# A projection stage whose written order is kept on VectorE alone, the other engines left to the list scheduler

## The chip, the core and the metric

The kernel runs on one core of a Trainium2 chip. Its time is the device time of one execution in microseconds (us). The engines are PE (TensorE: matmuls and transposes), DVE (VectorE), ACT (ScalarE), POOL (GpSimd) and SP (SyncE, which issues every DMA here). Each engine runs its own instructions in the order in which they stand in its program, and semaphores make one engine wait for another. So the time depends on two things that the arithmetic does not fix: the order on each engine, and what each instruction has to wait for.

## What is computed

One layer of a hybrid decoder trunk, for 2048 tokens of 1024 channels, in float32:

```python
mod = silu(c) @ W_ada + b_ada          # shift, scale, gate; for the mixer and for the MLP
h = rms_norm(x) * (1 + scale1) + shift1
p = h @ W_in                           # q_a k_a v_a | q_m k_m v_m o_m | u_s v_s | f_a i_m f_m
y = concat(forgetting_attention(q_a, k_a, v_a, f_a),       # 8 heads of 64
           sigmoid(o_m) * rms_norm(mlstm(q_m, k_m, v_m, i_m, f_m)),   # 4 heads of 64
           spatial_gating(gelu(u_s), gelu(v_s)))           # 4 groups of 64
x = x + gate1 * (y @ W_out)
x = x + gate2 * conv_ffn(rms_norm(x) * (1 + scale2) + shift2)
```

The change touches the product `h @ W_in` and the work that is done beside it.

## The kernel before

The program has four stages, one after another: the **projection** (`h @ W_in`, from the start to about 775 us), attention, the product with `W_out`, and the convolutional MLP.

**Precision.** A float32 operand is split into a rounded high part and a low rest (`hh` and `hl` of h, `wh` and `wl` of a weight), and `mm3` (lines 53 to 56) makes three matmuls of each product. The high part of a weight is a cast on ACT (line 652), the low part a subtraction on DVE (line 653).

**The projection's loop.** The list `steps` has 14 entries: seven blocks of columns of `W_in` for the first 1024 tokens, and the same seven for the other 1024. In the order of the first half they are `km` (keys of the mLSTM and all gates, 272 columns), `qo`, `vm`, `us`, `K`, `Q` and `V`. A block makes eight accumulators `acc` of 24 matmuls each, 112 in the whole stage; here they are counted from 0. They lie in three PSUM buffers, in the last step in two. While a block runs, the weights of the next are loaded (`wr`, three buffers, line 640 for the DMA) and split into `wh` and `wl` (eleven buffers each).

**The first block** (`first_block`, n = 0) is written apart, because h does not exist yet. x is loaded in tiles `xt` of 128 tokens; `norm_sums` squares each tile on ACT (line 558, two halves), sums on DVE (559, 561), takes a power on POOL (128), and line 571 scales the tile on DVE. `first_mod` sums the modulation on DVE (`modacc`, 442 and 444) and POOL (`modown`, 438 to 440) and transposes the sums on PE (447), and lines 453 to 455 give shift and scale for four of the eight channel tiles. `make_h` then goes over the eight channel tiles k: four transposes on PE (605), `h` on ACT (609), `hh` and `hl` on DVE (610, 611). Behind this block `mlstm_setup` (890 to 908) makes small constants: `sel`, `maskb`, `maskT`, `rmask`. `maskb` and `maskT` come from two POOL tiles (895 to 900).

**Side work.** From n = 1 on, generators ("lanes") hand out small pieces of other work between the products: the rest of the modulation (`rest_of_mod`, 500 and 502, with `columns_or_row`, 517 and 527), the recurrent mLSTM (`mlstm`, `mlstm_end`), the spatial gating (`level`, `spatial`), the transposes of normalised keys and queries (`turn`, 841 to 855: a sum, a power on POOL, `qn`, a transpose `trp`, then `qhi` and `qlo`), and for the second half a `refill` of the x tiles. In the last step (block `V`) the first eight attention scores run as a lane: `sp` on PE (206, 210), `L` with its minimum on DVE (212), an exponential on ACT (223). Block `V` itself evicts each accumulator in two halves, a cast on ACT (829) and a subtraction on DVE (830) into `vhl`, and stores them (831) from three buffers `q2k`.

**What sets the order.** Two mechanisms. A list scheduler places the instructions of an engine by its own estimate of when their inputs are ready; outside a `manual_schedule` it does so for all five. Inside `manual_schedule` (entered at n = 1 and left behind the loop) the engines named, that is PE, DVE, ACT and POOL, keep exactly the order in which the program is written, that is the order in which the lanes hand out their pieces. SP is not named, so DMAs are placed by the scheduler throughout. The first block lies outside and is placed by the scheduler on all engines.

Of the kernel before, what the change touches and what calls it, by code (L numbers as in the profile page):

```python
# [33 lines left out]
def trunk(  # L34
# [18 lines left out]
    def mm3(ps, lh, ll, rh, rl, start, stop, resume=False):  # L53
        T.matmul(ps, lh, rh, start=start, stop=False, skip_group_check=resume)  # L54
        T.matmul(ps, lh, rl, start=False, stop=False, skip_group_check=resume)  # L55
        T.matmul(ps, ll, rh, start=False, stop=stop, skip_group_check=resume)  # L56

# [417 lines left out]
    def rest_of_mod():  # L475
# [15 lines left out]
        for col in cols:  # L491
            acc = pool.tile([P, 512], F32, name="modacc", tag="t2k")
            for k in range(KT):
# [5 lines left out]
                if k == 0:  # L499
                    V.tensor_scalar(acc, st, cs[:, 0:1], None, op0=ALU.mult)  # L500
                else:
                    V.scalar_tensor_tensor(acc, st, cs[:, k : k + 1], acc, op0=ALU.mult, op1=ALU.add)
# [9 lines left out]
    def columns_or_row(acc, col):  # L512
# [4 lines left out]
        V.tensor_tensor(acc[0:1, :], acc[0:1, :], brow, op=ALU.add)  # L517
# [7 lines left out]
        else:  # L525
# [3 lines left out]
            if kind == 3:  # L529
                V.tensor_copy(sh2[:, sl], ps[:, 0:4])  # L530
            else:
                V.scalar_tensor_tensor(
                    a2[:, sl], ps[:, 0:4], 1.0, gf[:, half * 4 : half * 4 + 4], op0=ALU.add, op1=ALU.mult
                )
# [80 lines left out]
    class Weights:  # L615
# [28 lines left out]
        def cast(self):  # L644
# [8 lines left out]
            self.eng.tensor_tensor(lo, self.raw[k], hi.bitcast(F32), op=ALU.subtract)  # L653
# [74 lines left out]
    def use_km(tt, ps):  # L728
# [3 lines left out]
        V.tensor_tensor(gates[:, tt % 8, 64:72], ps[:, 256:264], gbias[:, 0:8], op=ALU.add)  # L732
        V.tensor_tensor(
# [3 lines left out]
        )  # L737
# [24 lines left out]
    def use_vm(tt, ps):  # L762
        t = pool.tile([P, 256], F32, name="ev", tag="ev")
        V.tensor_copy(t, ps[:, 0:256])
# [15 lines left out]
    def level(tt, i, t, u, vn):  # L780
        mu = pool.tile([P, 4], F32, name="mu", tag="mu")
        V.tensor_reduce(mu, t, axis=AX.X, op=ALU.add)
        V.tensor_scalar(mu, mu, 1.0 / 64, None, op0=ALU.mult)
        V.tensor_tensor(t, t, bc(mu, 2, 64), op=ALU.subtract)
# [12 lines left out]
    def spatial(tt, u, vn):  # L797
        y = pool.tile([P, 4, 256], F32, name="sy", tag="t4k")
        mixed = []
        for g in range(4):  # L800
# [6 lines left out]
            if g % 2:  # L807
                for g_ in (g - 1, g):
                    sl = slice(g_ * 64, g_ * 64 + 64)
                    V.tensor_tensor(y[:, :, sl], mixed[g_], bc(gsgu[:, sl], 1, 4), op=ALU.mult)  # L810
                    V.scalar_tensor_tensor(
                        y[:, :, sl], y[:, :, sl], bs_col[:, g_ : g_ + 1], u[:, :, sl], op0=ALU.add, op1=ALU.mult
                    )
# [11 lines left out]
    def use_v(tt, ps):  # L825
        for h0 in (0, 4):
# [3 lines left out]
            V.tensor_tensor(t[:, :, 1, :], p3, t[:, :, 0, :].bitcast(F32), op=ALU.subtract)  # L830
            dma(v_d[tt * P : (tt + 1) * P, h0 : h0 + 4], t.bitcast(F32).rearrange("p h e d -> p h (e d)"))

    def use_qk(which):
# [5 lines left out]
        def turn(tt, ps, sq):  # L839
            ss = pool.tile([P, 8], F32, name="ss", tag="ss")  # L840
            V.tensor_reduce(ss, sq.rearrange("p (h d) -> p h d", h=8), axis=AX.X, op=ALU.add)
            V.tensor_scalar(ss, ss, 1.0 / 64, EPS, op0=ALU.mult, op1=ALU.add)
# [1012 lines left out]
```

## Time and profile before

| What | Number |
|---|---|
| Median of 3 runs | 2672.68 us (2670.3 to 2673.54) |
| Profiled execution, its own time | 2675.71 us |
| Its span, from first to last instruction | 2674.0 us |
| Mean granted TensorE clock | 0.988 |

The rows of the profile are shown with the prediction, where they are used. Times in them are microseconds from the start of the span. A row of the timeline has the start, the duration, the engine, the line of the kernel, the operation, output and inputs by their names in the program, and in brackets the idle time of the engine ahead of it with the instruction that ended that idle time. A row of the windows has, for a stretch of time, the busy time of PE, its weight loads (PEld), DVE, ACT and POOL, each with its count of instructions, then the granted TensorE clock (1.00 is full), the share of time that the DMA engines were busy, and GB/s. A row of the waits says which engine waited at which line for which engine's result, for how long in all, how often, and at most.

### The profile page before, as it was taken

How to read it: one execution, taken by the hardware profiler on the slowest of the kernel's cores; microseconds unless marked ns; L12 is line 12 of the kernel's file. 1: busy time of each engine (PE TensorE's matmuls, PEld its weight loads, DVE VectorE, ACT ScalarE, POOL GpSimd, SP SyncE). 2: the span in 40 equal slices, each digit the busy share in tenths (PEclk: the TensorE clock that was granted, in tenths of full speed). 3: DMA queues.
4: the chain of work that ended last, by engine and by line, in shares of the span. 5: the costliest groups of instructions: out<-in, count | busy, mean ns of one | idle time of the engine just before them, and what ended most of it. 6: DMA issues, size and time to landing. Idle time of an engine off the chain costs nothing.

```text
span 2674.0 us, 36818 instructions
## 1 busy us (share of the span) xinstructions
PE 2580.6 (97%) x12761; PEld 2128.9 (80%) x12761; DVE 1992.1 (75%) x3432; ACT 1285.4 (48%) x2442; POOL 415.6 (16%) x550
## 2 busy tenths in 40 slices
PE   5899999999899999999999999999999999999999
PEld 5788787888777877777877888888888888888787
DVE  5555656455448888876749888887988887898797
ACT  3333334333248788874436544444444444444443
POOL 4012210022236566640000000000000000000000
PEclk9899999999999999999999999999999999999999
DMA  7533556424554444536742222228222225748533
GB/s 257 154 117 91 150 152 184 132 70 123 138 171 123 115 133 125 136 98 229 276 142 72 90 84 84 82 84 294 89 85 82 84 79 206 267 148 308 177 101 116
DMA packets 297683, 377.52 MB, mean 141 GB/s; under 512 B 31118, under 2 KB 189676, under 8 KB 295448
## 3 DMA queue, kind: packets, MB, share of 16 engines
q1 hardware_dynamic: 297496, 375.16, 44.4%
q8 instruction: 101, 1.65, 0.3%
q14 instruction: 86, 0.70, 0.1%
HBM read 274.34 MB, written 100.74 MB: 140 GB/s over the span
## 4 chain that ended last, share of the span: by engine, by line
PE 74%; DVE 11%; DMA 5%; ACT 4%; issue 4%; POOL 1%; SPq 0%; DVEq 0%; ACTq 0%; POOLq 0%
PE ub L54 10%; PE ub L56 10%; PE ub L55 10%; PE acc L54 5%; PE acc L56 5%; PE acc L55 5%; PE db L55 4%; PE db L56 4%; PE db L54 4%; PE tp L259 3%; PE sp L206 3%; PE op L245 2%; PE op L246 2%; DVE wspl L1599 2%; DMA x_d<-x 1%
## 5 line engine op out<-in xcount | busy, mean ns | idle before, releaser
L54 PE MATMUL acc<-wh,hh 128*128 128x512 f32 (+2 forms) x768 | 290.8, 379 | 10.9 <-DVE vhl L830 5.3
L55 PE MATMUL acc<-wl,hh 128*128 128x512 f32 (+2 forms) x768 | 277.5, 361 | 4.5 <-POOL wl L677 3.4
L54 PE MATMUL ub<-T,wsph 128*128 128x512 f32 x704 | 274.3, 390 | 5.8 <-ACT wsph L1467 5.8
L56 PE MATMUL acc<-wh,hl 128*128 128x512 f32 (+2 forms) x768 | 278.1, 362 | 0.4 <-DVE hl L611 0.4
L56 PE MATMUL ub<-T,wspl 128*128 128x512 f32 x704 | 273.8, 389 | 0.4 <-DVE wspl L1468 0.4
L55 PE MATMUL ub<-T,wsph 128*128 128x512 f32 x704 | 273.9, 389 | 0.0
L55 PE MATMUL db<-wspl,wsph 128*128 128x512 f32 x616 | 240.4, 390 | 2.2 <-DVE wspl L1599 2.2
L56 PE MATMUL db<-wsph,wspl 128*128 128x512 f32 x616 | 239.6, 389 | 0.0
L54 PE MATMUL db<-wsph 128*128 128x512 f32 x616 | 238.3, 389 | 0.3 <-ACT wsph L1598 0.3
L1467 ACT CAST wsph<-S 128x512 fp32r<-128x512 f32 x176 | 109.7, 623 | 228.6 <-PE ub L55 162.5
L263 DVE TENSOR_TENSOR plo<-tp,phi 128x512 fp32r<-128x512 f32 (+1 forms) x320 | 186.8, 607 | 35.9 <-ACT phi L262 34.0
L54 PE MATMUL ub<-B,wsph 128*128 128x512 f32 x528 | 207.3, 393 | 2.6 <-ACT wsph L1467 2.6
L56 PE MATMUL ub<-B,wspl 128*128 128x512 f32 x528 | 207.0, 392 | 0.8 <-DVE wspl L1468 0.8
L55 PE MATMUL ub<-B,wsph 128*128 128x512 f32 x528 | 207.1, 392 | 0.0
L223 ACT ACTIVATE L<-L,nm 128x1024 f32<-128x1024 f32 (+2 forms) x192 | 172.5, 902 | 32.1 <-DVE nm L212 30.8
L259 PE MATMUL tp<-ident,L 128*128 128x128 f32 x1088 | 178.6, 276 | 5.2 <-DVE vhl L830 1.9
L262 ACT CAST phi<-tp 128x512 fp32r<-128x512 f32 (+1 forms) x320 | 160.1, 521 | 46.0 <-PE tp L259 44.7
L54 PEld LDWEIGHTS acc<-wh,hh 128*128 128x128 f32 x768 | 148.3, 193 | 32.3 <-issue 6.6
L206 PE MATMUL sp<-kk,q 128*128 128x512 f32 (+3 forms) x640 | 168.4, 374 | 2.3 <-DVE nm L212 1.2
L228 POOL TENSOR_SCALAR L<-L,rs 128x1024 f32<-128x1024 f32 (+2 forms) x192 | 167.2, 881 | 11.2
L1598 ACT CAST wsph<-act 128x512 fp32r<-128x512 f32 x132 | 82.2, 623 | 179.0 <-PE db L55 162.6
L55 PEld LDWEIGHTS acc<-wl,hh 128*128 128x128 f32 x768 | 148.2, 193 | 25.1 <-POOL wl L677 3.7
(344 smaller groups left out, 6025.8 us busy)
## 6 DMA issues: line engine op xcount, KB each, us to landing
w<-in_w_up_dram SPq DMA_DIRECT2D x88, 512.0 KB
wd<-in_w_down_dram SPq DMA_DIRECT2D x176, 256.0 KB
wa<-in_w_ada_dram SPq DMA_DIRECT2D x96, 256.0 KB
act_d<-yc SPq DMA_DIRECT2D x44, 512.0 KB
act<-act_d SPq DMA_DIRECT2D x44, 512.0 KB
wr<-in_w_in_dram SPq DMA_DIRECT2D x76, 256.0 KB
q<-q_d SPq DMA_DIRECT2D x128, 128.0 KB
hc_d<-hl SPq DMA_DIRECT2D x28, 512.0 KB
```

The costliest lines, as they stand in the source:

```text
L54: T.matmul(ps, lh, rh, start=start, stop=False, skip_group_check=resume)
L55: T.matmul(ps, lh, rl, start=False, stop=False, skip_group_check=resume)
L56: T.matmul(ps, ll, rh, start=False, stop=stop, skip_group_check=resume)
L206: T.matmul(sp[:, b : b + bw], q2[n][:, qs], kk[:, s0 + b : s0 + b + bw], start=n == 0, stop=n == 1 and not last)
L223: A.activation(L[c], L[c], AF.Exp, bias=nm[:, n - 1 : n], scale=-1.0, accum_out=rs[:, c : c + 1])
L228: G.tensor_scalar(t, t, rs[:, 0:1], 1.0, op0=ALU.mult, op1=ALU.mult)
L245: T.matmul(op[:, c0:], vv[:, j, :], hi[:, c0:], start=(j == 0), stop=False)
L259: T.transpose(tp[:, i * P : (i + 1) * P], rows[i][j // 8][:, (j % 8) * P : (j % 8 + 1) * P], ident)
L262: A.copy(hi[:, c0:], tp[:, c0:])
L263: V.tensor_tensor(lo[:, c0:], tp[:, c0:], hi[:, c0:].bitcast(F32), op=ALU.subtract)
L1467: A.copy(hi, src)
L1598: A.copy(hi, v)
```

## The change

The `manual_schedule` goes. In its place most VectorE instructions of the projection are wrapped in `O(...)`, which ties an instruction behind the one that was written just before it on the same engine, whether that is wrapped or not. The scheduler then places PE, ACT and POOL freely through the whole projection, and DVE in written order as far as it is wrapped. Not wrapped are `make_h` (610, 611), `norm_sums` (559, 561), the scaling in `norm_x` (571), `mlstm_setup`, the copy in `small_setup` and the scores (212): these may move ahead of what is written before them. Since the wrapping also holds for the first block, some of its DVE instructions are now tied too. The sets of instructions are the same in both programs; behind the projection the order is the same too.

```diff
+    O = tc.keep_in_program_order
...
-                    V.tensor_scalar(acc, st, cs[:, 0:1], None, op0=ALU.mult)
+                    O(V.tensor_scalar(acc, st, cs[:, 0:1], None, op0=ALU.mult))
...
-            self.eng.tensor_tensor(lo, self.raw[k], hi.bitcast(F32), op=ALU.subtract)
+            O(self.eng.tensor_tensor(lo, self.raw[k], hi.bitcast(F32), op=ALU.subtract))
...
-        V.tensor_tensor(gates[:, tt % 8, 64:72], ps[:, 256:264], gbias[:, 0:8], op=ALU.add)
+        O(V.tensor_tensor(gates[:, tt % 8, 64:72], ps[:, 256:264], gbias[:, 0:8], op=ALU.add))
...
-            V.tensor_tensor(t[:, :, 1, :], p3, t[:, :, 0, :].bitcast(F32), op=ALU.subtract)
+            O(V.tensor_tensor(t[:, :, 1, :], p3, t[:, :, 0, :].bitcast(F32), op=ALU.subtract))
...
-            V.tensor_tensor(n, ps.rearrange("p (h d) -> p h d", h=8), bc(ss, 2, 64), op=ALU.mult)
+            O(V.tensor_tensor(n, ps.rearrange("p (h d) -> p h d", h=8), bc(ss, 2, 64), op=ALU.mult))
...
-    in_order = tc.manual_schedule(
-        engines={mybir.EngineType.PE, mybir.EngineType.DVE, mybir.EngineType.Activation, mybir.EngineType.Pool}
-    )
     for n, (half, i) in enumerate(steps):
         if n == 1:
-            in_order.__enter__()
             lane(in_turn(log_gates(), iter((6,)), small_setup()), 2)
...
-    in_order.__exit__(None, None, None)
```

The same wrapping stands around the VectorE lines of `columns_or_row`, `use_vm`, `level`, `spatial`, `turn`, `log_gates`, `mlstm`, `mlstm_end` and the scaling in `normed`. Lines behind 57 are two higher in the changed kernel.

**First place: the norms and the constants around the first block.** ACT before, from the second half's `h` to the squares. Tile numbers are the program's own: `xt_564` to `xt_570` are the x tiles 4 to 7, `acc_440`, `453` and `466` are accumulators 0, 1 and 2.

```order
L730 COPY ev_584<-acc_440 128x256
L730 COPY ev_604<-acc_453 128x256
L596 COPY wT_289<-mp_628 128x512
L730 COPY ev_649<-acc_466 128x256
L558 ACTIVATE jk_655,st_654<-xt_564 128x512
L558 ACTIVATE jk_657,st_654<-xt_564 128x512
L558 ACTIVATE jk_664,st_663<-xt_566 128x512
L558 ACTIVATE jk_666,st_663<-xt_566 128x512
L558 ACTIVATE jk_673,st_672<-xt_568 128x512
L558 ACTIVATE jk_675,st_672<-xt_568 128x512
L558 ACTIVATE jk_682,st_681<-xt_570 128x512
L558 ACTIVATE jk_684,st_681<-xt_570 128x512
```

ACT in the changed kernel at the same place; the same x tiles are `xt_562` to `xt_568`, the accumulators `438`, `451`, `464`, and `wr_599`, `644`, `713` are the first three raw weights of the next block.

```order
L654 CAST wh_837<-wr_599 128x512
L560 ACTIVATE jk_653,st_652<-xt_562 128x512
L560 ACTIVATE jk_655,st_652<-xt_562 128x512
L654 CAST wh_874<-wr_644 128x512
L654 CAST wh_911<-wr_713 128x512
L611 ACTIVATE h32_523<-mp_518,sh1_90,a1_89 128x512
L611 ACTIVATE h32_534<-trp_529,sh1_90,a1_89 128x512
L611 ACTIVATE h32_545<-trp_540,sh1_90,a1_89 128x512
L611 ACTIVATE h32_556<-mp_551,sh1_90,a1_89 128x512
L560 ACTIVATE jk_662,st_661<-xt_564 128x512
L598 COPY wT_289<-mp_626 128x512
L732 COPY ev_582<-acc_438 128x256
```

Three weight casts and the squares of x tiles 4 and 5 moved ahead of the `h` and the evictions; in the changed program four squares are left behind the third eviction (`ev_647`), where there were eight.

DVE before, at the end of the first block, with the constants of `mlstm_setup` between two low parts of weights:

```order
L653 TENSOR_TENSOR wl<-wr,wh 128x512 x4
L732 TENSOR_TENSOR gates<-acc,gbias 128x8
L733 TENSOR_TENSOR gates<-acc,gbias 128x2x4
L893 COPY sel<-ident 4x128 x4
L897 CAST maskb<-m_978 128x128
L901 CAST maskT<-maskf 128x512
L902 MEMSET rmask 4x512
L903 MEMSET rmask 4x4
L907 COPY sel<-ident 4x64 x4
L653 TENSOR_TENSOR wl<-wr,wh 128x512
```

DVE in the changed kernel, some fifty rows earlier: the last sums of the modulation (L444 and L446), and the masks between them.

```order
L444 TENSOR_SCALAR modacc<-wa,cs 128x512
L446 SCALAR_TENSOR_TENSOR modacc<-wa,cs,modacc 128x512 x6
L561 TENSOR_TENSOR st<-st 128x1
L899 CAST maskb<-m_976 128x128
L446 SCALAR_TENSOR_TENSOR modacc<-wa,cs,modacc 128x512
L563 TENSOR_SCALAR st<-st 128x1
L903 CAST maskT<-maskf 128x512
L446 SCALAR_TENSOR_TENSOR modacc<-wa,cs,modacc 128x512
L573 TENSOR_SCALAR xt<-xt,st 128x1024
L455 TENSOR_TENSOR sh_90<-mps,colA 128x4
L456 TENSOR_TENSOR a_89<-mps,colA 128x4
L457 SCALAR_TENSOR_TENSOR a_89<-a_89,colA 128x4
```

`maskb` and `maskT` moved ahead of the last two sums and of the shift and scale that `h` waits for; `rmask` and `sel` moved to the program's first rows. The scaling of x tile 4 (L573) moved ahead of the shift and scale too.

**Second place: the products behind the second set of transposes.** PE before, where accumulator 4 (`acc_811`) follows the last transpose of x:

```order
L605 MATMUL trp_800<-ident_74,xt_568 128x128
L605 MATMUL trp_800<-ident_74,xt_570 128x128
L54 MATMUL acc_811<-wh_346,hh_729 128x272
L55 MATMUL acc_811<-wl_347,hh_729 128x272
L56 MATMUL acc_811<-wh_346,hl_730 128x272
L54 MATMUL acc_811<-wh_352,hh_740 128x272
L55 MATMUL acc_811<-wl_353,hh_740 128x272
L56 MATMUL acc_811<-wh_352,hl_741 128x272
L54 MATMUL acc_811<-wh_358,hh_751 128x272
```

PE in the changed kernel, where `acc_809` and `acc_846` are accumulators 4 and 5:

```order
L607 MATMUL trp_798<-ident_74,xt_562 128x128
L607 MATMUL trp_798<-ident_74,xt_564 128x128
L607 MATMUL trp_798<-ident_74,xt_566 128x128
L607 MATMUL trp_798<-ident_74,xt_568 128x128
L54 MATMUL acc_809<-wh_364,hh_760 128x272
L55 MATMUL acc_809<-wl_365,hh_760 128x272
L56 MATMUL acc_809<-wh_364,hl_761 128x272
L55 MATMUL acc_846<-wl_347,hh_727 128x272
L54 MATMUL acc_809<-wh_370,hh_771 128x272
L55 MATMUL acc_809<-wl_371,hh_771 128x272
L56 MATMUL acc_846<-wh_346,hl_728 128x272
L54 MATMUL acc_846<-wh_352,hh_738 128x272
```

The matmuls of accumulators 4 and 5 now stand mixed with each other and with the transposes, as each channel tile of h is made. Before, accumulator 5 begins behind the last matmul of 4.

**Third place: the end of the projection.** PE before: `acc_6976` is accumulator 107 (block `V`), `sp_6990` the first attention score.

```order
L56 MATMUL acc_6976<-wh_6717,hl_3695 128x512
L54 MATMUL acc_6976<-wh_6748,hh_3745 128x512
L55 MATMUL acc_6976<-wl_6749,hh_3745 128x512
L56 MATMUL acc_6976<-wh_6748,hl_3746 128x512
L206 MATMUL sp_6990<-kk_6829,q_6835 128x512
L206 MATMUL sp_6990<-kk_6829,q_6838 128x512
L206 MATMUL sp_6990<-kk_6829,q_6835 128x128
L206 MATMUL sp_6990<-kk_6829,q_6838 128x128
L210 LDWEIGHTS identb_95
L210 MATMUL sp_6990<-maskb_97,identb_95 128x128
L54 MATMUL acc_6976<-wh_6757,hh_3769 128x512
L55 MATMUL acc_6976<-wl_6758,hh_3769 128x512
```

PE in the changed kernel: `acc_6941` is accumulator 106, `sp_6988` and `sp_7021` are the first two scores.

```order
L56 MATMUL acc_6941<-wh_6781,hl_3817 128x512
L54 MATMUL acc_6941<-wh_6806,hh_3827 128x512
L55 MATMUL acc_6941<-wl_6807,hh_3827 128x512
L56 MATMUL acc_6941<-wh_6806,hl_3828 128x512
L208 MATMUL sp_6988<-kk_6827,q_6833 128x512
L208 MATMUL sp_7021<-kk_6827,q_6833 128x512
L208 MATMUL sp_6988<-kk_6827,q_6836 128x512
L208 MATMUL sp_6988<-kk_6827,q_6833 128x128
L208 MATMUL sp_6988<-kk_6827,q_6836 128x128
L212 LDWEIGHTS identb_95
L212 MATMUL sp_6988<-maskb_97,identb_95 128x128
L208 MATMUL sp_7021<-kk_6827,q_6836 128x512
```

All eight scores, 40 rows, now stand between accumulators 106 and 107; before, each stood inside one of the accumulators 107 to 111, behind half of its matmuls.

DVE before, at the same place (L830 is the low half of an eviction of block `V`, L212 a score with its minimum, in two rows):

```order
L855 SCALAR_TENSOR_TENSOR qlo<-trp,gq_94,qhi 128x512
L830 TENSOR_TENSOR vhl<-acc,vhl 128x4x64 x2
L212 ISA L,nm<-sp,nf 128x640
L212 ISA nm 128x1
L830 TENSOR_TENSOR vhl<-acc,vhl 128x4x64 x2
L212 ISA L,nm<-sp,nf 128x768
L212 ISA nm 128x1
L212 ISA L,nm<-sp,nf 128x896
L212 ISA nm 128x1
L830 TENSOR_TENSOR vhl<-acc,vhl 128x4x64 x2
L212 ISA L,nm<-sp,nf 128x1024
L212 ISA nm 128x1
```

DVE in the changed kernel (L832 and L214 now):

```order
L214 ISA L,nm<-sp,nf 128x1024
L214 ISA nm 128x1
L214 ISA L,nm<-sp,nf 128x128
L214 ISA nm 128x1
L214 ISA L,nm<-sp,nf 128x256
L214 ISA nm 128x1
L214 ISA L,nm<-sp,nf 128x384
L214 ISA nm 128x1
L832 TENSOR_TENSOR vhl<-acc,vhl 128x4x64
L857 SCALAR_TENSOR_TENSOR qlo<-trp,gq_94,qhi 128x512
L832 TENSOR_TENSOR vhl<-acc,vhl 128x4x64
L214 ISA L,nm<-sp,nf 128x512
```

Rows 3 to 8 here are the last of seven scores that stand ahead of the second eviction half of accumulator 105 (L832 in row 9), behind which accumulator 107 finds its buffer free; before, evictions and scores took turns.

More of the change, by code (lines that the diff above doesn't have):

```diff
@@ L499, in rest_of_mod @@
                 if k == 0:
-                    V.tensor_scalar(acc, st, cs[:, 0:1], None, op0=ALU.mult)
+                    O(V.tensor_scalar(acc, st, cs[:, 0:1], None, op0=ALU.mult))
                 else:
-                    V.scalar_tensor_tensor(acc, st, cs[:, k : k + 1], acc, op0=ALU.mult, op1=ALU.add)
+                    O(V.scalar_tensor_tensor(acc, st, cs[:, k : k + 1], acc, op0=ALU.mult, op1=ALU.add))
                 if k == KT - 1:
@@ L516, in columns_or_row @@
         yield 2
-        V.tensor_tensor(acc[0:1, :], acc[0:1, :], brow, op=ALU.add)
+        O(V.tensor_tensor(acc[0:1, :], acc[0:1, :], brow, op=ALU.add))
         yield 1
@@ L809, in spatial @@
                     sl = slice(g_ * 64, g_ * 64 + 64)
-                    V.tensor_tensor(y[:, :, sl], mixed[g_], bc(gsgu[:, sl], 1, 4), op=ALU.mult)
-                    V.scalar_tensor_tensor(
+                    O(V.tensor_tensor(y[:, :, sl], mixed[g_], bc(gsgu[:, sl], 1, 4), op=ALU.mult))
+                    O(V.scalar_tensor_tensor(
                         y[:, :, sl], y[:, :, sl], bs_col[:, g_ : g_ + 1], u[:, :, sl], op0=ALU.add, op1=ALU.mult
-                    )
+                    ))
                 yield 1
@@ L926, in mlstm @@
         yield 1
[L927 to L929 removed]
+        O(V.tensor_copy(mp_[:, 0:1], mcar))
+        O(V.tensor_tensor_scan(m, lf, psI, mcar, op0=ALU.add, op1=ALU.max))
+        O(V.tensor_tensor_scan(b, rmask, lf, 0.0, op0=ALU.mult, op1=ALU.add))
         yield 1
[L931 to L935 removed]
+        O(V.tensor_tensor(e, m, b, op=ALU.subtract))
+        O(V.tensor_copy(mp_[:, 1:5], r4(m)[:, :, P - 1]))
+        O(V.tensor_tensor(a, psI, b, op=ALU.subtract))
+        O(V.tensor_tensor(r4(R[0:4]), bc(mp_[:, 0:4], 2, P), r4(e), op=ALU.subtract))
+        O(V.tensor_copy(mcar, mp_[:, 4:5]))
         A.mul(ne, e, -1.0)
@@ L1099, in normed @@
         scale = lambda pair, sts: [
-            V.tensor_scalar(xt, xt, st, None, op0=ALU.mult) for xt, st in zip(pair, sts)
+            O(V.tensor_scalar(xt, xt, st, None, op0=ALU.mult)) for xt, st in zip(pair, sts)
         ]
```

90 lines of the change are left out of this document (41 added, 49 removed).

## The prediction, made before the changed kernel ran

> **What bounds the kernel now.** First the page's totals and its chain, then windows by stage, then who waits on PE.
>
> ```profile
> span 2674.0 us, 36818 instructions
> PE 2580.6 (97%) x12761; PEld 2128.9 (80%) x12761; DVE 1992.1 (75%) x3432; ACT 1285.4 (48%) x2442; POOL 415.6 (16%) x550
> PE 74%; DVE 11%; DMA 5%; ACT 4%; issue 4%; POOL 1%; SPq 0%; DVEq 0%; ACTq 0%; POOLq 0%
> ...
> 0.00:100.00 100.00, 65.51 (x352) 57.59 (x353) 59.16 (x134) 40.22 (x89) 34.63 (x50) 0.91 0.59 198
> 100.00:750.00 650.00, 626.70 (x3395) 524.49 (x3395) 354.62 (x797) 221.57 (x435) 110.25 (x92) 0.98 0.46 135
> 750.00:800.00 50.00, 46.90 (x234) 36.88 (x233) 25.12 (x57) 24.47 (x57) 19.85 (x32) 0.97 0.54 158
> 800.00:2674.00 1874.00, 1841.48 (x8784) 1509.91 (x8782) 1553.24 (x2447) 999.09 (x1864) 250.89 (x376) 1.00 0.43 140
> ```
>
> PE is busy for 97% of the span and makes 74% of the chain that ends last. The change leaves every matmul in place, so it can only win or lose time in which PE is idle or at a lower clock. The first row of the windows (0 to 100 us) has 34.5 us of idle PE, the second (100 to 750) 23.3 us, at clock 0.98. From 800 us on the order is unchanged and PE runs at 1.00. So the whole effect lies in the first 780 us. What PE waits for there (0 to 800 us, the waits that the moved rows touch):
>
> ```profile
> PE acc L54 <- DVE vhl L830: 5.3, 2, 3.5
> PE acc L54 <- DVE qn L846: 5.1, 1, 5.1
> PE mp L521 <- DVE modacc L517: 3.9, 2, 2.2
> PE trp L850 <- DVE qn L846: 3.2, 2, 2.3
> PE acc L56 <- DVE wl L653: 2.3, 1, 2.3
> PE mp L527 <- DVE colC L551: 1.4, 1, 1.4
> PE acc L55 <- DVE wl L653: 1.0, 1, 1.0
> PE acc L54 <- ACT wh L652: 0.8, 1, 0.8
> ```
>
> They are short and scattered, and each is a place where one engine's order made a result late. There is no single large stall to remove.
>
> **First block, the start of h.** Three timelines, POOL, DVE and PE, around 50 us:
>
> ```profile
> 45.83 3.10 POOL L589 TENSOR_SCALAR_AFFINE_SELECT wsn<-wsn 128x128 f32<-128x128 f32 x4
> 70.91 0.20 POOL L895 MEMSET m<- 128x128 f32 x1
> ...
> 72.12 0.29 POOL L900 TENSOR_SCALAR_AFFINE_SELECT maskf<-maskf 128x128 f32<-128x128 f32 x1
> 43.70 5.08 DVE L444 SCALAR_TENSOR_TENSOR modacc<-wa,cs,modacc 128x512 f32<-128x512 f32 x5
> 58.39 0.40 PE L56 MATMUL acc<-wh,hl 128*128 128x272 f32 x1 [0.21 <-DVE hl L611]
> ```
>
> Here the change loses. `maskT` now stands on DVE ahead of the last modulation sum and needs POOL's four mask instructions, which took 70.91 to 72.41 = 1.5 us and come behind `wsn`, done at 48.93. So `maskT` can start at 50.4. With itself (0.4, below) and one sum (5.08 / 5 = 1.0) the sums end at 51.8 instead of 48.78, 3.0 late. Twelve of the sixteen transposes that stood between the sums and h are now ahead of them, which gives back about 0.8. I take h 2.2 us late: the last `hl` of these four channel tiles, at 58.3 before, comes at 60.5.
>
> **First block, the norms of the next x tiles.** DVE's first norm sum, its last scaling and the last `hl`; ACT's squares as groups (63 to 69 us); PE's first matmul of the next block:
>
> ```profile
> 64.96 0.16 DVE L559 TENSOR_TENSOR st<-st 128x1 f32<-128x1 f32 x1 [0.99 <-ACT jk L558]
> ...
> 71.00 0.75 DVE L571 TENSOR_SCALAR xt<-xt,st 128x1024 f32<-128x1024 f32 x1 [0.66 <-POOL st L128]
> ...
> 81.04 0.69 DVE L611 TENSOR_TENSOR hl<-h,hh 128x512 fp32r<-128x512 f32 x1
> L558 ACT ACTIVATE jk<-xt 128x512 f32<-128x512 f32 x8 | 4.9, 620 | 0.0
> L558 ACT ACTIVATION_READ_ACCUMULATOR jk<-xt 128x1 f32 x8 | 1.5, 191 | 0.0
> 91.05 0.40 PE L54 MATMUL acc<-hh,wh 128*128 128x512 f32 x1
> ```
>
> Before, eight squares of 0.8 with readout stand behind the third eviction, and four chains of sum, power and scaling follow each other from 64.96 to 71.75, 1.7 us each. PE, ACT and DVE then work through eight channel tiles until the last `hl` at 81.73. Now x tiles 4 and 5 are squared beforehand. The third eviction waits for the late `hl` at 60.5 and some ten matmuls, so it ends at about 62.6; four squares end at 65.9, and the last chain or, if two queue, both end between 67.6 and 69.3. I take 68.4: scaling 3.3 us earlier, the last `hl` at 78.4. Behind it stood 73 matmuls of 272 columns, the end of accumulator 4 and all of 5 to 7, until 91.05: 9.3 us, 0.127 each. Accumulator 5 is now mixed into the transposes, so 52 are left, 6.6 us. The block ends at 85 instead of 91, **6 us** earlier.
>
> **First block, the next weights.** DVE's constants, ACT's cast that waits for a load, PE's stall in the next block, the clock behind it and a window at full clock:
>
> ```profile
> 96.01 0.62 DVE L893 COPY sel<-ident 4x128 f32<-4x128 f32 x4
> ...
> 96.81 0.42 DVE L901 CAST maskT<-maskf 128x512 bf16<-128x512 f32 x1
> ...
> 98.43 0.67 DVE L653 TENSOR_TENSOR wl<-wr,wh 128x512 fp32r<-128x512 f32 x1
> 94.51 0.62 ACT L652 CAST wh<-wr 128x512 fp32r<-128x512 f32 x1 [4.24 <-DMA wr<-in_w_in_dram]
> 99.16 0.79 PE L56 MATMUL acc<-hh,wl 128*128 128x512 f32 x1 [2.29 <-DVE wl L653]
> ...
> 99.00:109.00 10.00, 9.84 (x31) 7.86 (x32) 6.88 (x16) 4.71 (x7) 0.00 (x0) 0.69 0.70 196
> ...
> 720.00:735.00 15.00, 13.12 (x60) 10.58 (x60) 3.38 (x7) 1.80 (x4) 1.64 (x1) 1.00 0.91 240
> ```
>
> The block does not continue when PE gets there: the eighth weight's low part is 2.29 us late, partly because 2.42 us of constants (96.01 to 98.43) stand in front of it on DVE. They are gone from there, and three weight casts are done long before, which also frees raw buffers for the next loads. The last weight needs a raw buffer that comes free some 6 us behind the last `hl`, at 84.5; its load takes about as long as ACT's wait of 4.24 us, and two casts and subtractions of 0.6 to 0.7 follow. My estimate is 91, so the matmul of 99.16 starts 8 us earlier. The bounds are 3.3 us (the weights follow the last `hl` as far behind as before, 99.16 - 81.73 = 17.4) and 8.9 (6 from the block, 2.29 from the stall and 0.6). Behind the stall PE ran at clock 0.69: 31 matmuls in 10 us. At the 0.22 to 0.23 of the window at full clock (13.12 / 60) those take 7, so 3 us more are won if no stall of that size is left, and 0 otherwise. First block: **8 + 3 = 11 us**, bounds 3 and 12.
>
> [...]
>
> **The middle, 100 to 710 us.** From the list of waits, each with the row that now comes earlier: `colC` (1.4) 0.5; the larger wait for `qn` before a transpose (2.3) 0.5, since `qn` no longer queues behind side work; the low weight (1.0) all; the cast (0.8) all, because next weights are now cast some 17 to 46 rows earlier on ACT; one of the two `modacc` waits 0.8; the 5.1 us for `qn` at the end of block Q 0.9. That sums to 4.5. I take **4 us**. The bounds are 9, when slow stretches such as this one also go,
>
> ```profile
> 280.00:300.00 20.00, 16.49 (x68) 12.46 (x67) 15.09 (x29) 8.47 (x14) 3.27 (x2) 0.91 0.69 206
> ACT wh L652 <- DMA wr<-in_w_in_dram: 54.4, 22, 7.3
> ```
>
> and minus 5, when some casts, which ACT already spends 54.4 us waiting for, now hold an eviction back behind a load.
>
> **The end, block V.** PE's first matmul behind its longest stall there and the window around it; the eight scores as groups of DVE and PE (740 to 775 us); SP's loads of the queries:
>
> ```profile
> 739.78 0.47 PE L54 MATMUL acc<-wh,hh 128*128 128x512 f32 x1 [3.46 <-DVE vhl L830]
> ...
> 735.00:745.00 10.00, 6.54 (x24) 4.97 (x23) 1.93 (x4) 1.59 (x4) 0.00 (x0) 0.83 0.88 270
> L212 DVE CUSTOM_DVE_ANT_0 L<-sp,nf 128x640 f32<-128x640 f32 (+7 forms) x8 | 6.0, 752 | 7.9 <-PE sp L210 7.9
> L206 PE MATMUL sp<-kk,q 128*128 128x512 f32 (+3 forms) x24 | 5.6, 340 | 0.0
> 723.93 8.71 SPq L173 DMA_DIRECT2D q<-q_d  x8
> ```
>
> PE stands still from 736.3 to 739.78, because an eviction buffer waits for its store, which SP issues only behind the loads for attention; then the clock is low. The eight scores now fill that stall. They need some 4.5 us of PE (24 matmuls, 5.6 us with overlap), but their two PSUM buffers come free only as DVE reads them. Eight reads make 6.0 us, and with the start and the handing over I take 7.3. So accumulator 107 starts near 743.6, not 739.78: 3.8 us lost, against 4.5 us of score matmuls that are then done and 1.7 us of low clock (0.17 of 10 us) that goes. Net **2.5 us won**. The bounds are 4 won, and 6 lost if the queries, issued until 732.64, land only near 744, where before the first score ran: every matmul of block V behind it waits too.
>
> **Sum.** 11 + 4 + 2.5 = 17.5. The profiled execution took 2675.71, so 2658.2. The median lies 3.03 below the profiled execution (2672.68 against 2675.71): **2655.2, given as 2656.**
>
> **Rivals.**
> *The weights set the pace.* The first block ends earlier, but the weights come 17.4 us behind the last `hl` as now. Then 3.3 is left of 11, and the stall moves to the new block end. With 1 of the middle and 0 at the end: 2672.7 - 4.3 = 2668.4, within the bound. For it speaks that three raw buffers and the loads' queue do not change; against it, that the constants do leave DVE and three casts are early.
> *ACT blocks on loads.* ACT runs in order, so a cast moved ahead of an eviction holds it until the weights land; the eviction holds an accumulator, and PE stops. Thirteen steps have such a cast. It decides from about 1.3 us of stall per step, which eats the 17.5: at 1.8 us in each it gives 23.4, so 2672.7 - 17.5 + 23.4 = 2678.6, slower. For it speaks the row of 54.4 us in 22 waits; against it, that accumulators have three buffers, 5.5 us of products each, and most moved casts have their load landed before in the trace.
> [...]
> *The order hardly changes what happens,* because semaphores set the same sequence anyway: 2672.7, with the weights' rival.
>
> **Chances and range.** Forecast 0.72; the weights or no effect 0.18; ACT on loads or the late queries 0.10. A measurement of this kernel can tell about 0.2% (5.3 us) from no change. Faster, below 2667.3: 0.74, with a little of the second case. Same 0.17. Slower 0.09. Lower bounds together (12, 9 and 4) give 2647.7; upper ones (3, a loss of 5 in the middle) about 2675. I take 2645 to 2674.
>
> **What would show it.** Right: the first matmul of `qo` at 85 and no stall over 2 us near 91 to 93, with clock near 1.00 there; scores between accumulators 106 and 107 with DVE L214 pacing them; from 800 us on the same length. Wrong: `wh` L654 waits on ACT with an eviction behind them, PE waits for evictions that were not there before, a first score that waits for `q`, or a last `hl` that is not earlier than 81.7.

## The result, and the profile after

| | Before | Changed |
|---|---|---|
| Median, same chip, 4 runs each | 2673.11 us (2670.30 to 2675.19) | 2648.39 us (2645.15 to 2652.26) |
| Ratio of the two, with its 95% interval | | 0.9909 [0.9891, 0.9927] |
| Profiled execution | 2675.71 us | 2645.15 us |

The change wins 24.7 us. The forecast was 2656 with a range of 2645 to 2674: the sign is right, the range holds, and the forecast is 7.6 us too slow. The two profiled executions differ by 30.6, because that of before lies 2.6 above its median and that of after is the fastest of its four. So some of each difference between these two traces is luck. A later run (`e3_first` below) has the same order of instructions as before, and its trace serves as a second sample. Another (`e5_nomid`) has that order until the last step and serves as a third.

The page of the changed kernel, its totals and its chain; then its windows, in the columns of before:

```profile
span 2643.4 us, 36797 instructions
PE 2562.8 (97%) x12745; PEld 2120.2 (80%) x12761; DVE 1988.1 (75%) x3432; ACT 1289.2 (49%) x2442; POOL 420.0 (16%) x550
PE 66%; DVE 9%; DMA 3%; issue 3%; ACT 2%; POOL 1%; SPq 0%; DVEq 0%; ACTq 0%; POOLq 0%
```

```profile
0.00:100.00 100.00, 70.13 (x388) 63.00 (x389) 61.92 (x142) 46.24 (x97) 33.63 (x50) 0.90 0.64 214
100.00:750.00 650.00, 634.32 (x3470) 533.49 (x3486) 357.04 (x812) 229.06 (x451) 125.17 (x108) 0.99 0.46 137
```

PE does more in the same time: 36 matmuls more in the first 100 us and 75 more in the next 650 (388 and 3470 against 352 and 3395), and it idles 15.7 us of the 650 where it idled 23.3.

What PE waits for in the first 800 us, the rows that answer to those of before:

```profile
PE acc L54 <- DVE qn L848: 3.7, 1, 3.7
PE trp L852 <- DVE qn L848: 3.0, 4, 1.0
PE acc L54 <- DVE vhl L832: 2.1, 2, 1.9
PE mp L523 <- DVE modacc L519: 1.4, 1, 1.4
PE sp L208 <- DMA q<-q_d: 1.2, 1, 1.2
PE sp L208 <- DVE nm L214: 1.2, 3, 0.7
PE acc L54 <- ACT wh L654: 0.4, 1, 0.4
PE acc L55 <- DVE wl L655: 0.2, 1, 0.2
```

None of the waits quoted before has grown. The rows of the scores (`sp`) were 0.2 each before. In the first block there is a new wait too, for `h` on ACT (3.6 and 1.0 us, not shown). The 2.3 us for `wl` are gone, one of the two `modacc` waits is gone, and where `qn` once cost a transpose 2.3 us the longest is now 1.0.

### Where the time went

Every accumulator `acc` begins with one matmul that both programs have, so its start can be compared. The first matmul of accumulators 10 and 96 before:

```profile
107.80 0.39 PE L54 MATMUL acc<-hh,wh 128*128 128x512 f32 x1
650.06 0.48 PE L54 MATMUL acc<-wh,hh 128*128 128x512 f32 x1
```

The same two in the changed kernel (rows 2 and 3), with the first of the second block (accumulator 8) ahead of them and that of 107 behind:

```profile
85.81 0.39 PE L54 MATMUL acc<-hh,wh 128*128 128x512 f32 x1
97.11 0.39 PE L54 MATMUL acc<-hh,wh 128*128 128x512 f32 x1
625.29 0.48 PE L54 MATMUL acc<-wh,hh 128*128 128x512 f32 x1
717.95 0.50 PE L54 MATMUL acc<-wh,hh 128*128 128x512 f32 x1 [0.25 <-DVE vhl L832]
```

Read in this way, in us, minus for earlier than in the profile of before:

| Kernel | acc 10 starts | acc 96 | acc 106 | acc 107 | acc 111 ends |
|---|---|---|---|---|---|
| the change | -10.7 | -24.8 | -25.9 | -21.8 | -29.0 |
| `e3_first`, the order of before | -2.1 | -3.9 | -3.3 | -3.2 | -3.1 |
| `e9_actfree`, ACT alone free | -2.1 | -15.0 | -17.5 | -19.5 | -21.1 |
| `e7_pefree`, PE alone free | -5.5 | -11.9 | -11.0 | -12.3 | -15.5 |
| `e10_dvefree`, DVE's untied rows alone | -6.4 | -8.4 | -7.7 | -9.4 | -11.0 |
| `e11_lolate` | -3.6 | -10.7 | -8.9 | -10.5 | -12.0 |
| `e5_nomid`, last step alone | -3.9 | -6.4 | -6.1 | -2.0 | -9.2 |
| `e1_pe`, PE pinned | -9.7 | -21.8 | -22.9 | -24.2 | -25.8 |
| `e2_act`, ACT pinned | -8.6 | -14.7 | -14.1 | -10.5 | -17.7 |
| `e6_free`, nothing tied | -11.9 | -17.9 | -25.0 | -22.2 | -28.3 |
| `e8_dve`, DVE wholly in order | -8.0 | -21.3 | -22.9 | -22.9 | -24.6 |
| `e12_const` | -10.7 | -24.8 | -27.4 | -23.3 | -30.5 |
| the change once more | -11.4 | -25.7 | -26.7 | -22.6 | -29.8 |

By the first row the first block with its weights won 10.7, the middle until accumulator 106 15.2, and the end 3.1. Against `e3_first` in place of before these are 8.6, 14.0 and 3.3, together 25.9, which is near the 24.7 of the medians. Against `e5_nomid`, which keeps the order of before until accumulator 106, the first two are 6.8 and 13.0. So the **middle** brought more than half of the gain, where the prediction had 4 us.

One order of instructions thus spreads over 3.9 us at accumulator 10 and 6.4 at 96, since the profile of before is the slowest of the three. A row that lies within that spread, such as that of `e10_dvefree`, says little by itself.

### The profile page after: what moved, and what is told of

The parts are those of the page before. It is cut to its first block, busy times and chain, and to the rows that moved or that the text cites. A ratio compares the mean times of both kernels' runs of the same rounds, so it can differ in the third digit from the quotient of the medians.

```text
span 2643.4 us, 36797 instructions
## 1 busy us (share of the span) xinstructions
PE 2562.8 (97%) x12745; PEld 2120.2 (80%) x12761; DVE 1988.1 (75%) x3432; ACT 1289.2 (49%) x2442; POOL 420.0 (16%) x550
## 4 chain that ended last, share of the span: by engine, by line
PE 66%; DVE 9%; DMA 3%; issue 3%; ACT 2%; POOL 1%; SPq 0%; DVEq 0%; ACTq 0%; POOLq 0%
PE ub L56 10%; PE ub L55 10%; PE ub L54 10%; PE db L55 4%; PE db L56 4%; PE db L54 4%; PE tp L261 3%; PE sp L208 3%; PE acc L54 3%; PE acc L56 3%; PE acc L55 3%; PE op L247 2%; PE op L248 2%; DVE wspl L1596 2%; PE wps L55 1%
## 5 line engine op out<-in xcount | busy, mean ns | idle before, releaser
L56 PEld LDWEIGHTS acc<-wh,hl 128*128 128x128 f32 x768 | 145.4, 190 | 21.5
```

## The experiments

Two theories stood at the start: that the gain is PE's (matmuls mixed, products moved beside transposes), or that it is ACT's (casts of the next weights placed early). Rivals gave the gain to the tie on DVE, to the first block alone, or to the end. POOL was never freed alone. Most kernels take the change and pin some engines again: an engine named here keeps the written order from the second block on. All ratios are against the kernel before on the same chip. In the diffs the engines' names are shortened.

### PE pinned, and ACT pinned

```diff
+    in_order = tc.manual_schedule(engines={PE})
     for n, (half, i) in enumerate(steps):
         if n == 1:
+            in_order.__enter__()
...
+    in_order.__exit__(None, None, None)
```

> The changed kernel with PE alone back in written order from the second block on; ACT and POOL stay with the scheduler, DVE as in the change. In the traces of before and of the change, PE's start of accumulator 10 is 10.7 us earlier, of accumulator 96 24.8 us, so the middle gave 14.1 us. Theory A (PE's own small swaps hide the waits of the middle): most of the 14.1 is lost and the scores are back inside the accumulators, so accumulator 96 starts 11 to 15 us earlier than in before and the time is 2658 to 2663. Theory B (earlier casts on ACT and multiplications on POOL make results come earlier): the middle stays, only the end's 3 us go, 2650 to 2653.

Measured: 2651.94, ratio 0.9925 [0.9906, 0.9944]. 20 us of the gain stay with PE in the written order, and accumulator 96 starts 21.8 us earlier than in before, not 11 to 15. So PE's swaps are not needed for most of it. The 4 us by which it is slower than the change are not clear of the intervals.

The second kernel has the same lines with ACT in place of PE:

```diff
+    in_order = tc.manual_schedule(engines={Activation})
```

> The changed kernel with ACT alone back in written order from the second block on. Theory A (PE's swaps): accumulator 96 still starts 22 to 25 us earlier than in before, time 2648 to 2653. Theory B (ACT's earlier casts): 10 to 14 us of the middle are lost, time 2658 to 2663.

Measured: 2657.33, ratio 0.9948 [0.9932, 0.9965]. Here the loss is larger: about 9 us of the 24 go with ACT's order, which lies between the two expectations. The middle until accumulator 96 wins 6.0 us where the change wins 14.1. But 15 us stay, so ACT isn't all of it either.

### All four pinned, and all four but for the last step

```diff
+    in_order = tc.manual_schedule(engines={PE, DVE, Activation, Pool})   # left behind the loop
```

> The changed kernel with PE, DVE, ACT and POOL in written order from the second block on, as in before: of the change only the first block is left. If the first block's gain stands by itself, accumulator 10 starts 10 to 11 us earlier than in before, nothing more is won behind it, and the time is 2661 to 2664. Rival: the gain hangs on casts that the scheduler moves ahead across the border of the first block (written order forbids these); then accumulator 10 is only 3 to 6 us earlier and the time 2667 to 2670.

Measured: 2671.92, ratio 0.9999 [0.9989, 1.0009]. Both expectations missed. Its instructions stand in exactly the order of before on every engine, in the first block too, although the wrapping in `O` is there. So the ties alone move nothing, and what moved in the first block moved because later blocks were free. That corrects a sentence ahead of the prediction: the first block is not free on its own.

```diff
+        if n == 12:
+            in_order.__exit__(None, None, None)   # only the last step is free
```

> The changed kernel with PE, DVE, ACT and POOL in written order from the second block up to the last but one; the first block and the last step (block V with the scores) are left to the scheduler as in the change. If the parts add up (first block 10.7, end 3): 2658 to 2661, that is 2 to 4 us below the run in which only the first block is left. Rival: the gain at the end exists only because of what was shifted before; then it equals that run within 1 us.

Measured: 2668.98, ratio 0.9984 [0.9971, 0.9996]. Less than expected; the pin holds the first block as well, so this kernel has the new end alone. Its row in the table shows it: accumulator 107 starts 4.1 us later against 106, and the last one ends 7.2 us earlier against 107. That is 3.1 us in the trace, and by the medians 2.9 under `e3_first`, with intervals that overlap. Neither expectation was met. That the new order at the end earns these 3 us is not shown, as the section on the prediction says.

### The tie on DVE: none, or complete

```diff
-    O = tc.keep_in_program_order
+    O = lambda i: i
```

> The changed kernel with nothing tied at all: VectorE is left to the scheduler too (340 of its instructions stand elsewhere than in the change). Theory: the written order on DVE keeps the short chains that PE waits for (weights, normalised q and k) ahead of side work; without it PE waits more for DVE and the time is 2652 to 2662, slower than the change by 4 us or more. Rival: the tie on DVE brings nothing, since semaphores keep the chain together anyway: 2646 to 2651.

Measured: 2648.33 against 2668.83, ratio 0.9922 [0.9904, 0.9941].

```diff
+    in_order = tc.manual_schedule(engines={DVE})
```

> The changed kernel with DVE alone in fully written order (the constants and the norms' scalings too); PE, ACT and POOL free. If the engines' gains add up (the change 24.7, without PE's freedom 20.1, without ACT's 14.7, each against the kernel before, so PE 4.6 and ACT 10), the rest of about 10 belongs to the few DVE instructions that moved ahead, above all the constants, and the time is 2656 to 2660. Rival: PE and ACT together have nearly all of it, the constants only fill idle time of DVE: 2649 to 2652.

Measured: 2647.66, ratio 0.9920 [0.9902, 0.9938]. Both times the rival was right: no tie at all and DVE wholly in written order give the same time within the intervals, and the change lies between them in what it ties. The tie that names the change makes no difference that was measured, though some 5 us to either side could hide in these intervals; what counts is that the other engines are free. The trace of `e6_free` shows a give and take behind that: PE waits 4.5 us once for a low part, accumulator 96 starts 7 us later than in the change, and at 106 the two are within 1 us again.

### One engine free at a time

ACT alone free, then PE alone (this one on the kernel before), then only what the change leaves untied on DVE:

```diff
+    in_order = tc.manual_schedule(engines={PE, DVE, Pool})          # e9
-        engines={PE, DVE, Activation, Pool}
+        engines={DVE, Activation, Pool}                             # e7
+    in_order = tc.manual_schedule(engines={PE, Activation, Pool})   # e10
```

> The kernel before with ACT alone left to the scheduler; PE, DVE and POOL in written order. If gains add up, ACT alone gives the 10 us that the change loses without it: 2660 to 2664, accumulator 96 about 9 us earlier than in before. Rival: ACT's early casts pay only together with the constants that leave DVE and the freed PE: 2667 to 2671.

Measured: 2657.11, ratio 0.9953 [0.9938, 0.9968], 11.7 us, more than expected. In the table it is level with `e3_first` until accumulator 10 and then wins 12.9 us until 96, where the change wins 14.1. So ACT alone is enough for most of what the middle won.

> The kernel before with PE alone left to the scheduler; DVE, ACT and POOL in written order. With PE, ACT and POOL free the ratio was 0.9920, with ACT alone 0.9953. If gains add up, PE brings the difference of 8 to 9 us alone: 2661 to 2665 where the kernel before has 2672. Rival: PE's swaps pay only when ACT no longer holds DVE back, so alone they bring 0 to 4 us: 2668 to 2672.

Measured: 2658.59 against 2670.74, ratio 0.9957 [0.9944, 0.9970], 12.2 us, more than expected. The rival, that PE's swaps are worth nothing alone, fell. Beyond `e3_first` it wins 3.4 us until accumulator 10, 4.6 until 96, 4.4 from there. ACT alone and PE alone sum to 23.9 of the change's 24, and yet pinning PE in the change cost only some 4 us (`e1_pe`), so the two gains overlap.

> PE, ACT and POOL in written order; on DVE only what the change wraps is tied, so the constants (sel, rmask, masks) and some norms move ahead (30 instructions). If gains add up, this gives 4 to 10 us: 2662 to 2668, with the 2.3 us stall in front of the second block's last weight gone, and the low clock behind it. Rival: the weight is late for its cast, not for the constants; then the stall stays over 1.5 us and the time is 2669 to 2673.

Measured: 2665.91, ratio 0.9981 [0.9971, 0.9991]. That is 2.9 us by the medians and 5.0 by the means, on which the ratio rests: little, but the time is in the expected range, and the wait that was to go did go. PE's matmul with the last weight of `qo`, in `e9_actfree` (DVE pinned):

```profile
98.25 0.80 PE L56 MATMUL acc<-hh,wl 128*128 128x512 f32 x1 [2.27 <-DVE wl L655]
```

The same matmul in `e10_dvefree`, where only 30 rows of DVE move, the constants among them:

```profile
92.28 0.39 PE L56 MATMUL acc<-hh,wl 128*128 128x512 f32 x1
```

The wait for the low part is gone. The constants and the norms moved together here, so which of them ended it is not separated.

### The mechanism in the middle

Why should ACT's casts matter when PE waited only 1.8 us for weights between 100 and 690 us? DVE's waits say it. The row of low parts waiting for their casts in that window, before, in the change, and with ACT alone free (total, times, longest):

```profile
DVE wl L653 <- ACT wh L652: 77.3, 39, 5.9
```

```profile
DVE wl L655 <- ACT wh L654: 17.5, 12, 2.7
```

```profile
DVE wl L655 <- ACT wh L654: 14.8, 11, 2.1
```

DVE keeps its order. Before, it stood for 77 us in front of subtractions whose cast had not come, and everything behind these in its queue stood too. With ACT pinned in the change (`e2_act`) the row is 73.9, with PE alone free 73.3, so it follows ACT's order.

Followed back along ACT's queue, 15.6 of the 77.3 us belong to casts that waited for their own load. Another 46.9 belong to casts that stood behind a square or an eviction, which had to wait for an accumulator; in the change these 46.9 are 6.7. One such place, ACT's timeline of before:

```profile
274.78 0.60 ACT L836 ACTIVATE qsq<-acc 128x512 f32<-128x512 f32 x1 [4.84 <-PE acc L56]
275.27 0.61 ACT L652 CAST wh<-wr 128x512 fp32r<-128x512 f32 x1
```

DVE's timeline of before, from the low part of that weight to `qn`:

```profile
275.92 0.69 DVE L653 TENSOR_TENSOR wl<-wr,wh 128x512 fp32r<-128x512 f32 x1 [3.02 <-ACT wh L652]
...
288.46 0.68 DVE L846 TENSOR_TENSOR qn<-acc,ss 128x512 f32<-128x512 f32 x1
```

and PE's timeline there, before and after:

```profile
289.29 0.84 PE L850 MATMUL trp<-ident,qn 128*128 128x128 f32 x4 [2.31 <-DVE qn L846]
```

```profile
274.22 0.63 PE L852 MATMUL trp<-ident,qn 128*128 128x128 f32 x4 [1.00 <-DVE qn L848]
```

PE's wait is booked to `qn`, and `qn` stands in DVE's queue behind a weight at which DVE had stood 3.02 us. But DVE waited twice more between the two (0.62 us at 277.23 and 0.23 us at 282.29, both for ACT). So why this wait is shorter in the change is left open. The path is plain at a sum of the modulation, where DVE waits for nothing between the weight and the sum. DVE's timeline of before:

```profile
463.47 0.44 DVE L653 TENSOR_TENSOR wl<-wr,wh 128x272 fp32r<-128x272 f32 x1 [2.17 <-ACT wh L652]
...
464.49 0.67 DVE L517 TENSOR_TENSOR modacc<-modacc,brow 1x512 f32<-1x512 f32 x1
```

and PE's:

```profile
465.31 1.10 PE L521 MATMUL mp<-modacc,ones 128*128 128x512 f32 x2 [1.71 <-DVE modacc L517]
```

PE's wait is booked to `modacc`, but DVE had just stood 2.17 us at a weight that has nothing to do with it. This cast had waited for its own load. The same matmul has no wait in the change (444.71) and with ACT alone free (454.09). To try this apart from ACT's order, the next kernel leaves every engine in written order and writes the low part later, behind the side work of the same slot (57 subtractions move on DVE; some loads are written later too):

```diff
-            self.eng.tensor_tensor(lo, self.raw[k], hi.bitcast(F32), op=ALU.subtract)
+            self.late = (lo, self.raw[k], hi)
...
         slot(w and i == 7)
+        if w:
+            w.rest()        # emits the subtraction kept in self.late
```

> The kernel before, all four engines in written order, with one thing moved: where a weight's cast and its low part are written in front of a piece of side work, the low part on DVE is written behind that piece (57 DVE instructions stand elsewhere; PE, ACT and POOL are as in before). Theory: in the middle DVE stands in front of low parts whose cast has not come (81.9 us of waits for it between 100 and 712 us, 17 with ACT free) and holds back the short chains of normalised q and k that PE waits for; then DVE's waits for casts fall below 45 us and the time falls by 4 to 8 us, 2664 to 2668. Rival: what pays is ACT itself, whose evictions and squares no longer queue behind casts; then the time stays within 2 us of before.

Measured: 2666.41, ratio 0.9986 [0.9977, 0.9995], 4.3 us. DVE's row and two of PE's, 100 to 690 us:

```profile
DVE wl L631 <- ACT wh L662: 20.2, 16, 3.0
```

```profile
PE acc L55 <- DVE wl L631: 2.7, 2, 2.5
PE acc L56 <- DVE wl L631: 1.5, 1, 1.5
```

The 77 us fell to 20 as the theory expects, and the time fell. The matmul of that sum of the modulation (458.97 here) has no wait any more, and the low part now stands behind the sum. The wait for `qn` stays, at 2.00 us, so it did not hang on these casts, though the expectation counted on such waits too. The interval reaches from 1.3 to 6.1 us, so by the time alone the rival's 2 us are not quite excluded. PE now waits 4.2 us for low parts that come too late, against 1.0 before, so 4.3 us may be what is left of a larger gain. In the middle (accumulators 10 to 96) it wins 7.2, and 5.4 beyond `e3_first`; ACT alone free wins 11.1 beyond it. So DVE standing in front of casts makes about a third of ACT's part by the medians (4.3 of 11.7) and half of it by the traces (5.4 of 11.1). What else brings the rest was not separated. SP's loads of weights, which the scheduler places, also stand elsewhere in `e9_actfree` and in `e11_lolate`, and no run kept them fixed.

The windows from accumulator 10 to accumulator 96 show in which form PE wins it. Before, with two stretches inside:

```profile
107.80:650.06 542.26, 530.20 (x2940) 445.91 (x2939) 305.10 (x695) 194.06 (x384) 89.82 (x80) 0.99 0.45 133
275.00:300.00 25.00, 21.49 (x93) 16.63 (x92) 18.50 (x33) 10.62 (x18) 3.27 (x2) 0.93 0.65 192
500.00:525.00 25.00, 22.64 (x156) 20.34 (x155) 16.79 (x35) 9.09 (x16) 0.00 (x0) 0.93 0.46 128
```

and the changed kernel, the same accumulators and one of the stretches:

```profile
97.11:625.29 528.18, 522.27 (x2925) 442.37 (x2939) 305.96 (x698) 195.20 (x382) 94.77 (x81) 1.00 0.46 137
275.00:300.00 25.00, 23.61 (x127) 18.84 (x127) 16.43 (x34) 9.10 (x21) 10.56 (x7) 1.00 0.60 176
```

Idle PE falls from 12.06 to 5.91, which is 6.1 us. Busy PE falls from 530.20 to 522.27, 7.9 us, for the same accumulators (`e3_first` had 528.22, so 6.0 is the difference to that run): that is mostly the clock, 0.93 in stretches behind a wait of 2.3 us (289.29) and one of 2.2 us (518.24), and 1.00 where these waits are 1.0 and 1.4. By the record of the granted clock before ran 10.2 us of these 542 at a clock of 0.5, `e3_first` 6.8 us, and the change none. A small part is not real: the trace of after lacks 15 matmul records here (2925 against 2940), and `e9_actfree`, with all of them and a clock of 1.00 too, has 523.63.

### The constants, and the change once more

The last kernel is the change with the setup of the constants tied behind accumulator 5 of the first block, so that `maskb` and `maskT` no longer stand ahead of the modulation's sums:

```diff
+            if i == 5:
+                mlstm_setup()      # its VectorE instructions wrapped in O(...)
```

> The change, with the small constants of mlstm_setup written behind the sixth accumulator of the first block and tied there, so that maskb and maskT no longer stand ahead of the last modulation sums. Theory: the sums end 2.5 to 3 us earlier than in the change (49.8 there), the last hl and the end of the first block 2 to 3 us earlier, the weights' low parts hardly later: 2 to 3 us faster than the change. Rival: the next weights' chain on DVE, behind the 2.4 us of constants, takes it back: within 1 us of the change.

Measured: 2645.30 against 2670.74, ratio 0.9906 [0.9890, 0.9921]. By the time the two expectations can't be told apart, since the change itself took 2646.94 on this chip (next run). DVE's shift and scale and the last weight, in this kernel:

```profile
52.33 0.16 DVE L457 SCALAR_TENSOR_TENSOR a<-a,colA 128x4 f32<-128x4 f32 x1
...
90.57 0.68 DVE L655 TENSOR_TENSOR wl<-wr,wh 128x512 fp32r<-128x512 f32 x1
```

In the change they stand at 53.28 and 90.58 (below). Scale and shift come 0.95 us earlier, not 2.5 to 3, and the last weight comes when it came, so it does not hang on h there. That speaks for the rival.

> The change itself once more, on the chip of this group, to compare the last run with: a ratio of 0.989 to 0.993 as before. All theories expect the same.

Measured: 2646.94, ratio 0.9918 [0.9903, 0.9933], on the chip of `e7`, `e11` and `e12`. The result repeats in runs of its own. `e12_const` beside it is not measurably faster, and no kernel of the study beats the change by more than the intervals.

## Why the prediction was right, and where its size was off

**First block: 11 predicted, 10.7 measured (8.6 beyond `e3_first`).** DVE's timeline after, from the masks to the last weight:

```profile
48.69 0.43 DVE L903 CAST maskT<-maskf 128x512 bf16<-128x512 f32 x1 [1.13 <-POOL maskf L902]
49.03 0.74 DVE L446 SCALAR_TENSOR_TENSOR modacc<-wa,cs,modacc 128x512 f32<-128x512 f32 x1
...
53.28 0.16 DVE L457 SCALAR_TENSOR_TENSOR a<-a,colA 128x4 f32<-128x4 f32 x1
...
67.31 0.75 DVE L573 TENSOR_SCALAR xt<-xt,st 128x1024 f32<-128x1024 f32 x1 [0.66 <-POOL st L130]
...
77.47 0.69 DVE L613 TENSOR_TENSOR hl<-h,hh 128x512 fp32r<-128x512 f32 x1
...
90.58 0.68 DVE L655 TENSOR_TENSOR wl<-wr,wh 128x512 fp32r<-128x512 f32 x1
```

`maskT` does wait for POOL, but from 48.69 and not 50.4, so the sums end at 49.77, 1.0 late and not 3.0: two of POOL's four mask instructions ran ahead of `wsn` and not behind it. The last `hl` of the four channel tiles still came at 60.54, as predicted (60.5), but for another reason. The copy `colA` (L398) now stands between these `hl`, and DVE waited 1.78 us there for a transpose on PE. That step was met by luck. The later ones came where they were put: last scaling done at 68.06 (68.4 predicted), last `hl` at 78.16 (78.4), `qo` from 85.81 (85), last weight at 91.26 (91). PE's matmul with that weight:

```profile
91.37 0.45 PE L56 MATMUL acc<-hh,wl 128*128 128x512 f32 x1
```

There is no stall, and the start is 7.8 us earlier, where 8 was predicted. The 3 us for the clock behind the old stall are the rest, 10.7 - 7.8 = 2.9, and that is luck in part. In `e3_first` the same stall had 7 slow matmuls behind it where before had 13 (from 100 to 125 us the clock was 0.96 there and 0.90 before), and in `e5_nomid` (2.17 us) none. So this term varies from one execution to the next, and the profile that the prediction was made from had the dearest of the three.

**The middle: 4 predicted, 14.1 measured until accumulator 96 and 15.2 until 106** (11.5 and 13.0 against `e5_nomid`). This is the term that was mis-sized. Its step added up PE's waits one by one (4.5 us) and priced only their idle time; that idle time did fall by 6.1. Two things were missing. The clock behind such waits was put into the bound of 9 and left out of the term, although the first block's term had it, and it gave most of the 7.9 us of busy time (6.0 against `e3_first`). And PE's waits were taken as separate accidents, while 77 us of DVE's waits, which the trace of before already held, were a common cause behind several of them. The bound of 9 fell too. The range still held, because the other terms stayed away from their best.

**ACT on loads.** This rival expected ACT to stand longer for loads and PE to pay. ACT's row for 100 to 690 us, before and after:

```profile
ACT wh L652 <- DMA wr<-in_w_in_dram: 45.1, 19, 7.3
```

```profile
ACT wh L654 <- DMA wr<-in_w_in_dram: 61.8, 37, 6.4
```

It does stand 16.7 us longer, and no eviction that PE waits for came late by it: PE's waits hold none of a product for an eviction on ACT. So its queue did stand at casts whose load had not come, as the rival had it, 61.8 us in 37 waits, but the cost fell on an engine that is busy 49% of the time.

**The end: 2.5 predicted, 3.1 measured, but not shown to come from the new order.** PE's first score and SP's loads of the queries, after:

```profile
710.24 1.02 PE L208 MATMUL sp<-kk,q 128*128 128x512 f32 x5
```

```profile
697.96 8.96 SPq L175 DMA_DIRECT2D q<-q_d  x8
```

From the first score to accumulator 107 (717.95) pass 7.7 us, where 7.3 was predicted, with short waits for DVE's `nm` (1.2 us in all) and for the queries (1.2, which the prediction had named as a sign of being wrong). Accumulator 107 loses 4.1 against 106 (3.8 predicted) and the rest wins 7.2 (4.5 + 1.7).

But `e11_lolate` has every engine in the order of before from 705 us on, with the scores inside the accumulators, and from accumulator 106 to the end of 111 it takes 40.7 us. The change takes 40.8 there, before 43.9 and `e3_first` 44.1. The stall of 3.46 us at accumulator 107 is 1.89 us in that run:

```profile
729.32 0.47 PE L54 MATMUL acc<-wh,hh 128*128 128x512 f32 x1 [1.89 <-DVE vhl L845]
```

So the old order too can do without the long stall, and a gain of 3 us is within what one order varies by. From the end of accumulator 111 on, the two programs take 1899.5 and 1898.0 us, the same length, as predicted. The rivals *weights set the pace* and *the order hardly changes* fell with the 24.7 us.

## What to carry to other kernels

On an engine that keeps its order, look not only at what the busiest engine waits for but at what the engine in front of it stands at: an instruction whose input comes from a third engine, placed too early, delays every unrelated result behind it. Free one engine at a time before you credit the edit that names a change; here the named tie was worth nothing that was measured, and two engines each won half alone, with overlap. Take more than one profile of the same order before you credit 3 us to an edit. And price a wait of PE with the clock behind it: here waits of 2.31 and 2.21 us became 1.00 and 1.40, and the clock of the stretches around them rose from 0.93 to 1.00 as well.

## What was not expected of the hardware

In these traces the granted clock was low behind waits of PE of little more than 2 us, and behind three shorter ones. The table has every wait of PE over 1.3 us between 80 and 790 us, in the profile of before and in that of the changed kernel, with the mean granted clock of the 10 us from its end.

| Profile | PE goes on at | Wait | Clock of the next 10 us |
|---|---|---|---|
| before | 99.16 | 2.29 us | 0.70 |
| before | 134.99 | 1.37 us | 0.83 |
| before | 289.29 | 2.31 us | 0.83 |
| before | 465.31 | 1.71 us | 1.00 |
| before | 518.24 | 2.21 us | 0.83 |
| before | 714.10 | 5.06 us | 0.72 |
| before | 724.71 | 1.88 us | 1.00 |
| before | 739.78 | 3.46 us | 0.83 |
| before | 776.40 | 1.92 us | 0.83 |
| changed | 495.99 | 1.40 us | 1.00 |
| changed | 687.91 | 3.68 us | 0.70 |
| changed | 698.76 | 1.88 us | 1.00 |
| changed | 747.36 | 1.92 us | 0.83 |

All six waits of the table over 2 us had a clock of 0.70 to 0.83 behind them. Of its seven from 1.37 to 1.92 us three had 0.83 and four 1.00, among them two of 1.88 with 1.00 and two of 1.92 with 0.83. While the clock was low, 512-column matmuls started 0.43 us apart (before, 715.08 to 715.94) instead of 0.23 (changed kernel, 718.28 to 718.98). One site of the changed kernel, PE's row and the window around it:

```profile
687.91 0.76 PE L54 MATMUL acc<-wh,hh 128*128 128x512 f32 x1 [3.68 <-DVE qn L848]
```

```profile
686.00:696.00 10.00, 8.09 (x25) 6.50 (x26) 3.10 (x6) 1.58 (x3) 0.00 (x0) 0.66 0.22 60
```

Not every long wait had a low clock behind it. In `e9_actfree` one of 3.50 us left the clock at 1.00, PE's row and the window around it:

```profile
697.48 0.47 PE L54 MATMUL acc<-wh,hh 128*128 128x512 f32 x1 [3.50 <-DVE qn L848]
```

```profile
695.00:705.00 10.00, 6.17 (x28) 4.82 (x28) 4.53 (x9) 2.89 (x6) 1.64 (x1) 1.00 0.44 120
```

So in these traces the length of a wait alone did not tell the clock behind it, and what else decides was not shown. No run varied the gap by itself.
